# Head norms raised to a power on GpSimd, and later places for three returned inverses, in a hybrid decoder layer

## The chip, the cores and the metric

The kernel runs on one core of one Trainium2 chip. The time is device microseconds of one execution. The kernel before was timed in three runs: 1850.33, 1848.37 and 1849.48 us, median 1849.48.

## The reference

One layer of a decoder, for a prompt of 256 tokens and 8 single sampled tokens (264 columns in all), width 2048: a SwiGLU feed-forward net, a mixing layer, a second feed-forward net, and a final norm. The mixing layer projects to 38 blocks of 128 columns; half of its heads do sliding-window attention, the other half RWKV-7 time mixing: per head a state matrix that is carried from token to token.

```
    S, y = wkv_scan(wkv0, r, logw, k, v, kk, a)
    mean = jnp.mean(y, axis=-1, keepdims=True)
    var = jnp.mean((y - mean) ** 2, axis=-1, keepdims=True)
    yn = ((y - mean) * lax.rsqrt(var + GN_EPS)).reshape(B, T, RWKV_WIDTH) * ln_w + ln_b
    ...
    out = (yn + bonus.reshape(B, T, RWKV_WIDTH)) * g
```

The change concerns `rsqrt(var + GN_EPS)` of these 16 heads, which the kernel handles as 8 pairs of heads, each a tile of 128 partitions by 264 columns.

## The kernel before

Every large product (both feed-forward nets, the projections `win`, the output `wout`) goes through `gemm` (L154). It takes the weights in chunks of up to four 128x128 blocks. A chunk (L136) is loaded by SP into `raw`, rounded by ACT into `hi`, and the rest is taken by VectorE (DVE) into `lo`; TensorE (PE) then does three matmuls of 264 columns for each block, into a bank called `acc`. There are seven buffers each of `raw`, `hi` and `lo`, so that ACT and DVE can be at most seven chunks ahead of PE. The chunks run 1 to 1312 over the program: 544 in the first net, 152 for the 38 blocks of `win`, 16, 32 and 32 in the three passes of `wout`, 536 in the second net.

All else in the mixing layer is written as generator tasks. After each chunk of `win` and `wout` a `tick` (L96) advances every living task by one `yield`, so that their small instructions are spread between the chunks:

- `prep` (L450): one pair of heads, from the projections to the 64x64 blocks `gm`.
- `chain` (L577): one batch of two pairs, four batches in all (0 to 3). It inverts triangular 32x32 matrices by 30 steps on DVE (tiles `X`, `Xt`, `st`), sends the result through memory (`sb`) into the tile `TT`, waits `RWAIT` ticks (L616), transposes `TT` on DVE into `TN` (L620), builds the 64x64 inverses, walks the four chunks of time (tiles `N`, `Z`, `S`), and ends with the norms.
- `gnorm` (L744): the norm of a pair: on PE the centred `y`, ACT squares it, PE sums the squares, ACT takes the square root (L752), DVE the reciprocal (L753), and DVE multiplies (L754). Two more DVE operations with weight, bias, bonus and gate follow (L739, L740).
- `attend` (L790) and `dec_attend`: the attention heads, with softmax over DVE (maximum, reciprocal), ACT (exponential) and GpSimd (POOL; a product at L787).

DVE's instructions in a tick keep the order in which the program writes them (L57 to L62): a DVE instruction of one task that waits holds up those of all tasks behind it. The instructions of `chunk` are exempt when they are written with high priority (L138); Tile's scheduler decides where they and all other instructions stand on each engine's queue, by its own reckoning of when operands are ready. After that each engine works its queue strictly in order.

Before a pass of `wout` (L958) the heads that it needs have to be done: pass 0 takes batches 0 and 1, pass 1 four attention heads' tiles and batch 2, pass 2 batch 3 and the other four. The matmuls of a pass need the `hi` and `lo` of these (`split`, L947: `s<-y` and `s<-o`).

Of the kernel before, what the change touches and what calls it, by code (L numbers as in the profile page):

```python
# [9 lines left out]
AF = mybir.ActivationFunctionType  # L10
ALU = mybir.AluOpType
AX = mybir.AxisListType

P = 128
NP = 256
NB = 8
T = NP + NB
# [13 lines left out]
NWARM = 7  # L31
NGM, NKR, NUV, NTT, NBT = 10, 5, 3, 2, 5
NSTEP = 2
DWAIT, RWAIT = (10, 9, 8, 8), (12, 11, 9, 10)
PW = (2, 1, 3, 2, 2)
ALPHA = math.exp(-0.5)
LKV = 26
# [10 lines left out]
def body(tc, I, O):  # L48
    nc = tc.nc
    A, G, TE, SP = nc.scalar, nc.gpsimd, nc.tensor, nc.sync  # L50
# [13 lines left out]
    V, inside = Ordered(), [False]  # L64

    def tt(e, out, a, b, op):
        return e.tensor_tensor(out=out, in0=a, in1=b, op=op)  # L67
# [4 lines left out]
    def ts(e, out, a, s1, op0, s2=None, op1=None):  # L72
        k = {} if op1 is None else dict(op1=op1)
        e.tensor_scalar(out=out, in0=a, scalar1=s1, scalar2=s2, op0=op0, **k)

    def act(out, in_, f, **k):
        return A.activation(out=out, in_=in_, func=f, **k)  # L77

    def bc(ap, shape):
        return ap.broadcast_to(list(shape))  # L80

    def mm(out, lhsT, rhs, start=True, stop=True, **k):
        TE.matmul(out, lhsT, rhs, start=start, stop=stop, **k)  # L83
# [27 lines left out]
    def pause(n):  # L111
        for _ in range(n):
            yield

    with ExitStack() as ctx:
# [10 lines left out]
        def tmp(shape=(P, T), dt=F32):  # L126
            pool, n = cur[0]
            return pool.tile(list(shape), dt, tag="t", bufs=n, name=uid("t"))
# [4 lines left out]
        def mp():  # L133
            return pp.tile([P, 512], F32, tag="m", bufs=NM, name=uid("m"))
# [38 lines left out]
        eps = cp.tile([P, 2], F32, name="eps")  # L173
# [209 lines left out]
        def mixing(n2, n3, XD):  # L383
            with tc.tile_pool(name="mx", bufs=1) as mx:
                cur[0] = (mx, NT)
                return mixing_body(mx, n2, n3, XD)

        def mixing_body(mx, n2, n3, XD):
            def fix(shape, name):
                return mx.tile(list(shape), F32, name=name)  # L390
# [18 lines left out]
                G.memset(pj[:, 0:1], 0.0)  # L409
            nmu = fix((P, NSH), "nmu")  # L410
            mu = vec[:, VMU:VMU + NSH]
            nka = fix((P, NPAIR), "nka")
            ts(G, nka, vec[:, VKA:VKA + NPAIR], -1.0, ALU.mult)
            ts(V, nmu, mu, -1.0, ALU.mult, 1.0, ALU.add)
# [162 lines left out]
            def chain(bt):  # L577
# [10 lines left out]
                for g in range(ng):  # L588
                    r = slice(g * nr, (g + 1) * nr)
# [81 lines left out]
                for k in range(n):  # L671
                    for c in range(1, 4):
                        x = (k * 3 + c - 1) * 64
                        for h in range(2):
                            r = HALF[h]
                            mm(pP[HALF[1 - h], x:x + 64], W[r, k, c - 1, :], bt.BT[k][r, c, r])
                        for h in range(2):
                            r = HALF[h]
# [7 lines left out]
                for k in range(n):  # L686
                    for c in range(4):
                        x = (k * 4 + c) * 64
                        for h in range(2):
                            r = HALF[h]  # L690
                            mm(pN[r, x:x + 64], bt.BT[k][:, c, r], uv[:, c, k, r])
                for k in range(n):
                    for c in range(4):
                        x = (k * 4 + c) * 64
                        for h in range(2):
                            r = HALF[h]
# [7 lines left out]
                for c in range(1, 4):  # L704
                    ps = mp()
                    for k in reversed(range(n)):
                        for h in range(2):
                            r = HALF[h]
                            mm(ps[r, k * 64:k * 64 + 64], PT[r, k, c - 1, :], S[r, k])
                        for h in range(2):  # L710
                            r = HALF[h]
# [16 lines left out]
                g2s = [load(I["g2"][bt.p0 + k], (P, P)) for k in range(n)]  # L728
                gps = []
                gs = [gnorm(Ys[k]) for k in range(n)]  # L730
                for _ in range(PW[3] + 1):
                    for g in gs:
                        next(g)
                    yield
# [9 lines left out]
            def gnorm(y):  # L744
                yp = mp()
                mm(yp[:, :T], cm, y)
                r = tmp()
                act(r, yp[:, :T], AF.Square)
                yield from pause(PW[3])
                vp = mp()  # L750
                mm(vp[:, :T], bo, r)
                act(r, vp[:, :T], AF.Sqrt, scale=1.0 / 64, bias=eps[:, 1:2])  # L752
                V.reciprocal(r, r)  # L753
                tt(V, y, yp[:, :T], r, ALU.mult)  # L754
                yield

# [150 lines left out]
            for kind, i in SEQ:  # L907
                if kind == "b":
                    bt = newbatch(i)
                    for k in range(BATCH[i]):  # L910
                        p = bt.p0 + k
                        x = [shifted(2 + 3 * p + j, tmp()) for j in range(3)]
                        spawn(prep(p, bt, k, *x))
                    bat.append(spawn(chain(bt)))
                    bts.append(bt)
                    if len(bat) == len(BATCH):
# [209 lines left out]
```

## Time and profile before

| | us |
|---|---|
| median of three runs | 1849.48 |
| the profiled execution, its own time | 1849.28 |
| its span in the profile | 1847.5 |
| PE busy | 1823.9 |
| DVE busy | 1317.1 |
| ACT busy | 1068.6 |
| POOL busy | 258.7 |

The profile is one execution; its time is 0.2 us from the median, and 1.8 us of it lie outside of the span. A group's row gives line, engine, operation, output and inputs by name, shapes, count, then busy time and mean ns of one, then the idle time of the engine just before them and what ended it. A row of windows gives for a stretch (from:to, us) its length, the busy time and number of instructions of PE, PEld (weight loads), DVE, ACT and POOL, the granted clock of PE (1.00 is full), the DMA share and GB/s. Line 60 is the helper through which all DVE operations go, line 77 that of ACT's functions, line 67 that of `tensor_tensor` on POOL, line 83 that of matmuls: groups are told apart by their tiles.

### The profile page before, as it was taken

Reading aid. Unit: us, or ns where it says so; the run is one execution under the profiler, and the core shown is the slowest. Engines: PE = TensorE matmul, PEld = TensorE weight load, DVE = VectorE, ACT = ScalarE, POOL = GpSimd, SP = SyncE. Lnnn points to the kernel's source line nnn. Section 1 sums busy time; section 2 is a strip of 40 time slices with the busy share of each in tenths; the row PEclk is TensorE's granted clock in tenths of the full one; section 3 lists DMA queues with packets and bytes.
Section 4 is the critical chain, followed back from the end, with each engine's and each line's share of the span. In section 5 each row is a group of like instructions: output and inputs, shape, how many; then the busy total and the mean of one; then the engine's idle time right before and its main releaser. Section 6 shows DMA issues by size and latency. Waiting matters only on the chain.

```text
span 1847.5 us, 46195 instructions
## 1 busy us (share of the span) xinstructions
PE 1823.9 (99%) x17212; PEld 1795.0 (97%) x17212; DVE 1317.1 (71%) x2613; ACT 1068.6 (58%) x2134; POOL 258.7 (14%) x389
## 2 busy tenths in 40 slices
PE   9999999999999999999998999999999999999998
PEld 9999999999999999999997899999999999999997
DVE  6966666666656677799887687876766676667765
ACT  6645555455554567877766676654545555454555
POOL 0401001010010122222221200220101001010012
PEclk9999999999999999999999899999999999999999
DMA  8666666666666677555566356666666666666664
GB/s 274 191 204 211 196 212 205 202 198 188 205 190 201 196 203 241 177 169 152 164 177 177 118 148 213 186 201 190 203 206 208 195 208 205 203 207 193 215 190 137
DMA packets 226466, 358.25 MB, mean 194 GB/s; under 512 B 38441, under 2 KB 82113, under 8 KB 226241
## 3 DMA queue, kind: packets, MB, share of 16 engines
q1 hardware_dynamic: 220352, 349.20, 62.7%
q10 hardware_dynamic: 5888, 6.11, 1.1%
q8 instruction: 135, 2.21, 0.5%
q14 instruction: 91, 0.74, 0.1%
HBM read 347.06 MB, written 10.22 MB: 193 GB/s over the span
## 4 chain that ended last, share of the span: by engine, by line
PE 93%; DVE 2%; DMA 2%; issue 1%; ACT 1%; SPq 0%; POOL 0%; POOLq 0%; ACTq 0%; DVEq 0%
PE acc L83 85%; PE m L83 7%; DVE lo L60 1%; DMA raw<-in_gu 0%; DMA raw<-in_wout 0%; DMA sb<-Xt 0%; ACT t L77 0%; DVE t L60 0%; DMA X<-sa 0%; DMA TT<-sb 0%; DVE st L60 0%; ACT hi L147 0%; DVE Xt L60 0%; PE m L551 0%; DMA raw<-in_win 0%
## 5 line engine op out<-in xcount | busy, mean ns | idle before, releaser
L60 DVE TENSOR_TENSOR lo<-raw,hi 128x512 fp32r<-128x512 f32 (+2 forms) x1312 | 884.5, 678 | 439.9 <-ACT hi L147 410.9
L147 ACT CAST hi<-raw 128x512 fp32r<-128x512 f32 (+2 forms) x1312 | 775.9, 596 | 665.8 <-PE acc L83 446.7
L83 PE MATMUL acc<-s,hi 128*128 128x264 f32 x5940 | 1034.1, 278 | 3.4 <-ACT s L950 2.2
L83 PEld LDWEIGHTS acc<-s,hi 128*128 128x128 f32 x5940 | 901.1, 189 | 9.5 <-ACT s L950 2.6
L83 PE MATMUL acc<-s,lo 128*128 128x264 f32 x2970 | 824.3, 278 | 0.2 <-DVE lo L60 0.2
L83 PEld LDWEIGHTS acc<-s,lo 128*128 128x128 f32 x2970 | 562.2, 189 | 2.3 <-DVE lo L60 0.4
L83 PE MATMUL acc<-t,hi 128*128 128x264 f32 x2752 | 465.0, 276 | 0.0
L83 PEld LDWEIGHTS acc<-t,hi 128*128 128x128 f32 x2752 | 414.9, 189 | 0.0
L83 PE MATMUL acc<-t,lo 128*128 128x264 f32 x1376 | 379.2, 276 | 0.0
L67 POOL TENSOR_TENSOR t<-t,t 128x264 f32<-128x264 f32 (+1 forms) x148 | 140.6, 950 | 1068.7 <-ACT hi L147 986.0
L83 PEld LDWEIGHTS acc<-t,lo 128*128 128x128 f32 x1376 | 260.1, 189 | 0.0
L83 PE MATMUL acc<-y,hi 128*128 128x264 f32 x648 | 113.8, 277 | 0.0
L83 PEld LDWEIGHTS acc<-y,hi 128*128 128x128 f32 x648 | 97.8, 189 | 0.2
L83 PE MATMUL acc<-y,lo 128*128 128x264 f32 x324 | 89.4, 276 | 0.0
L60 DVE TENSOR_TENSOR t<-acc,t 128x264 f32<-128x264 f32 x156 | 67.3, 431 | 20.4 <-PE acc L83 12.0
L67 POOL TENSOR_TENSOR o<-o,o 128x264 f32<-128x264 f32 x43 | 35.9, 835 | 198.7 <-ACT o L77 192.6
L83 PEld LDWEIGHTS acc<-y,lo 128*128 128x128 f32 x324 | 61.2, 189 | 0.0
L83 PE MATMUL acc<-o,hi 128*128 128x264 f32 x324 | 58.8, 276 | 0.0
L83 PEld LDWEIGHTS acc<-o,hi 128*128 128x128 f32 x324 | 48.8, 189 | 0.0
L60 DVE SCALAR_TENSOR_TENSOR s<-acc,s 128x264 f32<-128x264 f32 x96 | 40.9, 430 | 8.9 <-PE acc L83 6.3
L300 ACT CAST t<-t 128x264 fp32r<-128x264 f32 x86 | 38.5, 447 | 13.5 <-POOL t L67 8.1
L83 PE MATMUL m<-s,hi 128*128 128x264 f32 x260 | 44.9, 277 | 0.2
(243 smaller groups left out, 1276.3 us busy)
## 6 DMA issues: line engine op xcount, KB each, us to landing
raw<-in_gu SPq DMA_DIRECT2D x680, 256.0 KB, 3.4
raw<-in_dn SPq DMA_DIRECT2D x224, 256.0 KB, 3.0
raw<-in_win SPq DMA_DIRECT2D x152, 256.0 KB, 3.6
raw<-in_dn SPq DMA_DIRECT2D x160, 192.0 KB, 2.7
raw<-in_wout SPq DMA_DIRECT2D x48, 256.0 KB, 3.3
raw<-in_wout SPq DMA_DIRECT2D x32, 128.0 KB, 2.5
s<-xsp SPq DMA_DIRECT2D x16, 132.0 KB, 3.5
raw<-in_gu SPq DMA_DIRECT2D x16, 128.0 KB, 3.3
```

Of the source, the lines that this page charges most:

```text
L60: i = getattr(nc.vector, name)(*a, **k)
L67: return e.tensor_tensor(out=out, in0=a, in1=b, op=op)
L83: TE.matmul(out, lhsT, rhs, start=start, stop=stop, **k)
L147: A.copy(hi[:, :w], raw[:, :w])
L300: A.copy(halves(hi), pairs(u))
```

## The change

The norm's variance gets its epsilon by a plain ACT operation (Identity: scale and bias), and GpSimd raises it to the power of -0.5, with a constant tile `half` that is read with stride zero. The square root and the reciprocal are gone. Between the power and DVE's product stand three more ticks, and the loop that drives the norms is three ticks longer. `RWAIT`, the ticks between the return of the inverses' diagonal blocks and their transposition, grows by 1, 2 and 8 for batches 1, 2 and 3.

```diff
-DWAIT, RWAIT = (10, 9, 8, 8), (12, 11, 9, 10)
+DWAIT, RWAIT = (10, 9, 8, 8), (12, 12, 11, 18)
...
+            half = fix((P, 1), "half")
+            G.memset(half, -0.5)
...
-                for _ in range(PW[3] + 1):
+                for _ in range(PW[3] + 4):
                     for g in gs:
                         next(g)
                     yield
...
-                act(r, vp[:, :T], AF.Sqrt, scale=1.0 / 64, bias=eps[:, 1:2])
-                V.reciprocal(r, r)
+                act(r, vp[:, :T], AF.Identity, scale=1.0 / 64, bias=eps[:, 1:2])
+                tt(G, r, r, bc(half, (P, T)), ALU.pow)
+                yield from pause(3)
                 tt(V, y, yp[:, :T], r, ALU.mult)
```

Over the whole program the built kernel has 8 reciprocals fewer on DVE, 9 loads of a function table fewer on ACT, and on POOL 8 `TENSOR_TENSOR t<-t,half` more (and one memset); PE and SP have the same instructions. What moves is their order. Three places show it. Line numbers of the changed kernel are two to three higher behind the edits.

On DVE before, behind the sums of squares of batch 0 (the pairs 0 and 1 have the tiles `y_13237` and `y_13238`; their variances are `t_13619` and `t_13623`; `lo` is the rest of a weight chunk):

```order
L60 TENSOR_TENSOR lo_14043<-raw_14041,hi_14042 128x512
L60 RECIPROCAL t_13619<-t_13619 128x264
L60 TENSOR_TENSOR lo_14093<-raw_14091,hi_14092 128x512
L60 TENSOR_TENSOR y_13237<-m_13617,t_13619 128x264
L60 RECIPROCAL t_13623<-t_13623 128x264
L60 TENSOR_TENSOR lo_14127<-raw_14125,hi_14126 128x512
L60 SCALAR_TENSOR_TENSOR y_13237<-y_13237,vec,t_11146 128x264
L60 TENSOR_TENSOR st_13935<-X_13683,Xt_13684 128x30
L60 TENSOR_TENSOR y_13238<-m_13621,t_13623 128x264
```

On DVE in the changed kernel, the second of these two products (its pair's tile is now `y_13240`) and what stands around it:

```order
L60 TENSOR_TENSOR lo_16524<-raw_16522,hi_16523 128x512
L60 TENSOR_TENSOR lo_16550<-raw_16548,hi_16549 128x512
L60 SCALAR_TENSOR_TENSOR o_16327<-acc_16181,rs 128x264
L60 TENSOR_TENSOR lo_16581<-raw_16579,hi_16580 128x512
L60 TENSOR_TENSOR y_13240<-m_13623,t_13625 128x264
L60 SCALAR_TENSOR_TENSOR t_13748<-t_13748,t_13747 128x264
L60 SCALAR_TENSOR_TENSOR y_13240<-y_13240,vec,t_11516 128x264
L60 TENSOR_TENSOR t_13748<-t_13748,t_13744 128x264
L60 SCALAR_TENSOR_TENSOR y_13240<-y_13240,vec,m_13855 128x264
L60 TENSOR_TENSOR st_13937<-X_13685,Xt_13686 128x30
```

Before, the first product stands behind chunk 648 and the second behind chunk 649, and the tasks go on at once (`st`, the inversion of batch 2). Now the first stands behind chunk 677 and the second behind chunk 703, and with it everything that the tasks still have for DVE: the inversion `st_13937` of batch 2, which stood three rows behind the first product, comes only here. Behind chunk 703 there are 126 DVE instructions in a row with no `lo` between them, behind chunk 719 there are 130, behind chunk 751 there are 21.

On PE before, the end of the last block of `win` and the start of pass 0 (`s_16405` is a split head):

```order
L83 MATMUL acc_16188<-s_10600,hi_16333 128x264
L83 MATMUL acc_16188<-s_10601,hi_16333 128x264
L83 MATMUL acc_16188<-s_10600,lo_16334 128x264
L83 MATMUL m_15904<-t_15745,s_14845 64x256
L83 MATMUL m_15904<-t_15809,s_14845 64x256
L83 MATMUL m_15904<-t_15746,s_14845 64x128
L83 MATMUL m_15904<-t_15810,s_14845 64x128
L816 MATMUL m_15932<-C,t_15756 128x128
L817 MATMUL m_15932<-C,t_15755 128x128
L818 MATMUL m_15932<-C,t_15755 128x128
L83 MATMUL acc_16421<-s_16405,hi_16423 128x264
```

On PE in the changed kernel, the end of the same block, and then the end of what stands ahead of pass 0 (149 rows of this stretch are left out):

```order
L83 MATMUL acc_16181<-s_10600,lo_16311 128x264
L83 MATMUL m_13943<-t_13820,C 128x280
L83 MATMUL m_13946<-XD,ld_13872 64x2 x2
...
L83 MATMUL m_14768<-t_14678,C 128x264
L83 MATMUL m_14772<-t_14682,C 128x264
L767 MATMUL m_14833<-C,s_14793 8x128
...
L83 MATMUL m_15033<-s_14339,o_14978 128x256
L83 MATMUL m_15033<-s_14339,o_14978 128x128
L83 MATMUL acc_16377<-s_16361,hi_16379 128x264
L83 MATMUL acc_16407<-s_16361,hi_16409 128x264
```

Before, 7 small matmuls stand between the last block of `win` and pass 0; now there are 243, from the preparation of pair 6 to the norms of batch 1. Ahead of them the 48 chunks that end with this block stand on PE without a single small matmul between them, where before small ones stood between almost all of them.

On DVE, the transposition of batch 3's returned inverses before, and that of batch 2's in the changed kernel:

```order
L60 RECIPROCAL stb_15761<-stb_15761 128x2
L60 STREAM_TRANSPOSE TN_16235<-TT_14798 32x256
L60 TENSOR_TENSOR stb_15819<-stb_15819,stc_15820 128x2
L60 RECIPROCAL stb_15819<-stb_15819 128x2
L60 TENSOR_TENSOR stb_15873<-stb_15873,stc_15874 128x2
L60 STREAM_TRANSPOSE TN_16235<-TT_14798 32x256
```

```order
L60 TENSOR_TENSOR Xt_13686<-Xt_13686,st_14687 128x8
L60 TENSOR_TENSOR gm_14641<-m_14631,C 128x512
L60 TENSOR_TENSOR gm_14690<-m_14632,C 128x512
L60 STREAM_TRANSPOSE TN_15073<-TT_13695 32x256 x2
L60 TENSOR_TENSOR s_14887<-acc_14795,rs 128x264
L60 TENSOR_TENSOR s_16362<-y_13239,s_16361 128x264
L60 TENSOR_TENSOR s_16366<-y_13240,s_16365 128x264
L60 TENSOR_TENSOR y_14289<-m_14676,t_14678 128x264
```

In the first, the transposition stands among the attention's softmax (`stb`). In the second, it stands two instructions behind the last step of the inversion (`Xt_13686`) whose result it is to read after the trip through memory, and ahead of the products of batch 1 (`y_14289`) that pass 0 needs. In ticks, batch 3's transposition goes from tick 150 to 158 and the end of its norms from 163 to 174, where pass 2 begins with tick 200.

## Prediction

> **What bounds the kernel now.** The page comes first: the shares of the engines and the chain that ended last.
>
> ```profile
> PE 1823.9 (99%) x17212; PEld 1795.0 (97%) x17212; DVE 1317.1 (71%) x2613; ACT 1068.6 (58%) x2134; POOL 258.7 (14%) x389
> PE 93%; DVE 2%; DMA 2%; issue 1%; ACT 1%; SPq 0%; POOL 0%; POOLq 0%; ACTq 0%; DVEq 0%
> ```
>
> PE works all the time, so an operation that leaves DVE or ACT is worth nothing by itself; time can only come from PE's 23.6 us of idleness, its clock, or be lost by making PE idle. The windows over the mixing layer's second half show where it idles.
>
> ```profile
> 885.00:1007.50 122.50, 119.63 (x1524) 109.95 (x1522) 105.79 (x326) 85.99 (x213) 25.14 (x50) 1.00 0.61 173
> 1007.50:1017.50 10.00, 2.20 (x12) 1.19 (x11) 4.56 (x26) 6.47 (x21) 1.71 (x4) 0.72 0.70 202
> 1017.50:1104.00 86.50, 85.80 (x946) 77.23 (x947) 64.64 (x196) 58.69 (x163) 14.21 (x28) 0.95 0.43 128
> 885.00:1104.00 219.00, 207.63 (x2481) 188.38 (x2480) 174.99 (x546) 151.15 (x397) 41.06 (x80) 0.97 0.55 157
> 1020.00:1030.00 10.00, 10.00 (x71) 8.32 (x69) 6.13 (x25) 5.64 (x18) 2.44 (x7) 0.72 0.30 87
> ```
>
> One hole, ahead of pass 0, holds 7.8 us of the idleness, and the clock stays low behind it. The timeline names the waits.
>
> ```profile
> 1014.40 0.47 PE L816 MATMUL m<-C,t 128*128 128x128 f32 x1 [5.25 <-ACT t L788]
> 1016.00 0.43 DVE L60 STREAM_TRANSPOSE TN<-TT 32x256 f32<-32x256 f32 x1 [3.57 <-DMA TT<-sb]
> 1017.53 1.03 PE L83 MATMUL acc<-s,hi 128*128 128x264 f32 x3 [2.23 <-ACT s L950]
> 1018.21 0.44 DVE L60 STREAM_TRANSPOSE TN<-TT 32x256 f32<-32x256 f32 x1 [1.48 <-DMA TT<-sb]
> ```
>
> DVE stands at batch 3's transposition, whose data is still on its way; softmax and the splits for pass 0 queue behind it, and PE waits for these. The edit of `RWAIT` aims at this hole.
>
> **The change, part by part.** The rows of what goes, and of what is nearest to what comes:
>
> ```profile
> L60 DVE RECIPROCAL t<-t 128x264 f32<-128x264 f32 x8 | 14.4, 1800 | 5.4 <-ACT t L77 5.4
> L77 ACT ACT_TABLE_LOAD x27 | 34.6, 1283 | 2.4 <-PE m L83 1.9
> L77 ACT ACTIVATE t<-m,eps 128x264 f32<-128x264 f32 x8 | 3.6, 480 | 0.1
> L67 POOL TENSOR_TENSOR t<-t,t 128x264 f32<-128x264 f32 (+1 forms) x148 | 140.6, 950 | 1068.7 <-ACT hi L147 986.0
> L60 DVE TENSOR_TENSOR y<-m,t 128x264 f32<-128x264 f32 x8 | 3.4, 424 | 0.0
> ```
>
> *Removed:* 8 x 1.80 = 14.4 us of DVE and 9 x 1.28 = 11.5 us of ACT; the ACT function itself stays (0.48 us, taken as equal). Neither engine is the bound, so this counts only inside stretches where PE waits for them.
>
> *Added:* 8 powers on POOL. No row shows one. Below: POOL's product of the same size, 0.95 us. From the nearest kind: DVE's reciprocal takes 1.80/0.424 = 4.2 times its product, and a power is a logarithm, a product and an exponential; at 4.2 products for each of the two functions it is 2 x 4.2 x 0.95 + 0.95 = 9 us. No row bounds it above; 32 us is the point at which the first pair of powers would be late too (two of them in the 66 us of the first stage below), and serves as the upper end. I take 9 us and keep 1 and 32.
>
> The Trainium skill (GPSIMD Engine Reference, 3.1) gives about 2.6 cycles for each element of a two-input operation on GpSimd and calls VectorE the right engine for elementwise work; if a power ran at that rate it would be an estimated 264 x 2.6 / 1.2 GHz = 0.6 us, and the sum below would be that of the cheap power. The trace agrees on products (0.95 against 0.42 us) and says nothing on powers.
>
> *Moved:* this decides. The queues shown above with the change say that DVE's product of batch 0's second pair now stands behind chunk 703, seven chunks into pass 0. The seven buffers let DVE get there only when PE has done the last chunk of `win`, and pass 0 itself needs batch 1, which stands behind that product. So the small work that was spread over the chunks now stands in three heaps, ahead of the three passes, with no chunk to fill PE meanwhile: 126, 130 and 21 DVE instructions (ACT: 94, 81, 13 between two casts), with the DMAs on SP that go between. That holds whatever a power costs, as each engine's order is fixed.
>
> The sum goes by stages from 885 us, where batch 0's variances are ready, to 1104 us, where pass 2 starts. For the small instructions I take the stretch's mean without the chunks' own:
>
> ```profile
> 0.00:885.00 885.00, 444.12 (x647) 1.00 0.67 200
> 885.00:1104.00 219.00, 64.86 (x103) 0.97 0.55 157
> 885.00:1104.00 219.00, 58.32 (x104) 0.97 0.55 157
> ```
>
> These are the `lo` on DVE up to 885 us (647 chunks) and after, and the `hi` on ACT: DVE (174.99 - 64.86)/(546 - 103) = 0.249 us for each small instruction, ACT (151.15 - 58.32)/(397 - 104) = 0.317 us, a `lo` 0.63 us. PE's pace, its pace behind the hole, and the trip through memory are in the chain of waits:
>
> ```profile
> 1099.57 39.38 PE acc L83 x350
> 1023.75 2.05 PE acc L83 x10
> 1011.07 3.04 DMA sb<-Xt
> 1015.58 2.60 DMA TT<-sb
> ```
>
> A matmul takes 39.38/350 = 0.1125 us, and 0.205 behind the hole.
>
> 1. The 49 chunks left of `win`, nothing between: 49 x 12 x 0.1125 = 66 us.
> 2. First heap: DVE alone 126 x 0.249 = 31 us; if DVE and ACT (94 x 0.317 = 30) took turns, 61. In it batch 1 goes from PE to ACT to DVE a dozen times, while batch 2's inversion and two preparations fill in: midway, 46. Batch 2's transposition now waits for its whole trip, 3.04 + 2.60 us, ahead of batch 1's products: 52. Ends 31 and 67.
> 3. Pass 0: 192 matmuls are 22 us, but DVE has 92 x 0.249 + 16 x 0.63 = 33 us. Ends 33 and 38.
> 4. Second heap (batch 2 and most of the attention): 130 x 0.249 = 32 us; in turns with ACT's 26 us, 58. Midway 45.
> 5. Pass 1: 288 matmuls 32 us, and some small ones between: 38. Ends 32 and 42.
> 6. Third heap: 5 us; in turns, 9: 7.
>
> Together 66 + 52 + 33 + 45 + 38 + 7 = 241 us against 219 now: +22. The hole of now is in the 219, so its end is in this; the added ticks of `RWAIT` bring nothing more, for ticks are worth time only while chunks run between them, and batch 2's transposition stands two instructions behind the end of its inversion. Batch 3's is now off PE's way. The later ends (batch 1 at tick 121, 2 at 143, 3 at 174) lie ahead of the passes (152, 168, 200), and cost nothing by themselves.
>
> PE's clock: today's hole costs some 4 us behind it (2.8 us in 1020 to 1030 at 0.72, and about half of the 2.5 us ahead of that). Three holes instead of one: +8. The Trainium skill (TensorE: Matmul & The Clock Gate, Part 1) has the clock halve after an idle window of about 3.4 us and come back after a busy one; the hole shows it (5.25 us idle, then 0.72). By this rule of the Trainium skill alone, heaps that keep PE ticking over with small matmuls might keep the clock, and the sum would be 8 us less.
>
> The powers: in each heap two follow each other on POOL ahead of the product that the pass waits for, 2 x 9 = 18 us, of which the trip of batch 2's inverses covers 6 in the first, and DVE's other rows 2 each in the others: 54 - 10 = +44.
>
> Sum: 1849.3 + 22 + 8 + 44 = **1923 us** by the profiled execution (1849.28, the median being 1849.48); rounded to 1925. For the range: with a power of 1 us, all covered, 1879; of 32 us, 1849.3 + 30 + 192 - 10 = 2061; all lower ends (66 + 31 + 33 + 32 + 32 + 5 = 199) without clock or powers 1829; all upper ends (66 + 67 + 38 + 58 + 42 + 9 = 280), clock, cheap power 1918.
>
> **The rivals.**
>
> *A cheap power.* POOL is idle 86% of the span and its products take under a microsecond; nothing on ACT or DVE has to wait for it then. Only the heaps are paid: 1879 us. For it: the one POOL row of this shape. Against: that row is a product.
>
> *A dear power: POOL is the bound.* At 32 us or more each, six of the eight stand in PE's way, one after the other: 2061 us, and 6 to 8 us more for each further microsecond. For it: between the variances and their products the new order leaves 29 and 26 chunks, as if much time were needed there; that is no time, but it is odd for a cheap operation. It decides from about 20 us on (1989 us).
>
> *Faster: the heaps run dense.* DVE has 20% of this stretch idle today, and the reciprocals go from it. If in the heaps DVE hardly ever waited, these took 69 us, and the whole stretch 199 instead of 219: 1829 us. It decides where the three heaps need less than 219 - 66 - 33 - 38 = 82 us, that is, DVE busy over 69/82 = 84% in them, with a cheap power. It has 80% today, with chunks to fill in; in the heaps there is none, and the steps of a batch wait for each other over three engines and a DMA trip. I hold it unlikely.
>
> *The change does what it says but its places don't:* this is in the sum, since the order shows it.
>
> **How the numbers follow.** A power of 4 to 20 us: 0.40 (the forecast, 1893 to 1989). Cheap: 0.24 (1855 to 1893). Dear: 0.26. Dense: 0.10. The range reaches from the cheap case's lower edge, 1855, to a power of some 38 us, 2095; that leaves out the dense case and the dearest tenth. A time within 0.2% (3.7 us, about what a measurement of this kernel can tell from no change) needs a stretch of 215 to 223 us: 0.04, from the seam of dense and cheap. Faster 0.08, slower 0.88.
>
> **What would show it.** In the profile after: some 66 us of PE from about 885 us on with nothing but `acc`; then a hole ahead of each pass in which PE does only small matmuls, at a lower clock, the first 40 to 70 us long; in the rows, POOL `t<-t,half` with its mean, and DVE's `y<-m,t` waiting for POOL twice the power's length. Wrong if the holes are missing or under 82 us together, or if the order on the chip spreads the small work over the chunks as before; the size stands or falls with the mean of the power.

## The result, and the profile after

The changed kernel takes 2128.87 us (median of 4 runs, 2127.17 to 2131.41), the kernel before on the same chip 1849.74 us (4 runs, 1848.37 to 1850.33): 1.1512 times as long, 95% interval 1.1499 to 1.1526. The forecast was 1925, with a range up to 2095.

The page of the kernel after: span, engines, the bars of PE, POOL and PE's clock, and the chain that ended last.

```profile
span 2128.4 us, 46202 instructions
PE 1854.7 (87%) x17212; PEld 1815.8 (85%) x17212; DVE 1305.0 (61%) x2605; ACT 1061.8 (50%) x2125; POOL 593.6 (28%) x398
PE   9999999999999999996234183199999999999998
POOL 1201010101011222493976927802110110101012
PEclk9999999999999999996667587599999999999999
PE 80%; POOL 8%; issue 6%; DVE 3%; DMA 1%; ACT 1%; SPq 0%; POOLq 0%; ACTq 0%; DVEq 0%
```

The span grew by 280.9 us. PE has the same 17212 matmuls, and its busy time grew by only 31 us; so most of the loss is idleness of PE. The bars of PE and POOL are mirror images from slice 19 to slice 26, counted from 1 (a slice is 53 us): the fuller POOL is, the emptier is PE. POOL, which had 0% of the chain before, now has 8% of it, some 170 us.

The groups of instructions of the kernel after; L67 is POOL's power, L60 DVE's product with it, L953 the split for a pass, L83 the pass's matmuls:

```profile
L67 POOL TENSOR_TENSOR t<-t,half 128x264 f32<-128x264 f32 x8 | 339.9, 42498 | 39.8 <-ACT t L77 39.6
L60 DVE TENSOR_TENSOR y<-m,t 128x264 f32<-128x264 f32 x8 | 3.5, 431 | 238.6 <-POOL t L67 238.6
L953 ACT CAST s<-y 128x264 fp32r<-128x264 f32 x8 | 3.2, 430 | 110.4 <-DVE y L60 109.6
L83 PE MATMUL acc<-s,hi 128*128 128x264 f32 x5940 | 1032.9, 279 | 76.5 <-ACT s L953 75.9
```

One power takes 42.5 us, 8 of them 339.9. DVE's eight products took 0.43 us each and stood idle 238.6 us ahead of them, all of it for the power; before, the same row had no idle time. Behind three of the late products the split waits on ACT (109.6 us), and PE on the split (75.9 us); behind the others PE waits for DVE directly. That is the chain of the loss, link by link; the waits of its links overlap and are not added.

The timeline of the kernel after shows the powers on POOL (start, length; two rows in one are two powers back to back) ...

```profile
883.88 42.47 POOL L67 TENSOR_TENSOR t<-t,half 128x264 f32<-128x264 f32 x1 [2.02 <-ACT t L77]
927.22 42.78 POOL L67 TENSOR_TENSOR t<-t,half 128x264 f32<-128x264 f32 x1
1013.40 84.85 POOL L67 TENSOR_TENSOR t<-t,half 128x264 f32<-128x264 f32 x2 [6.43 <-ACT t L77]
1139.88 42.47 POOL L67 TENSOR_TENSOR t<-t,half 128x264 f32<-128x264 f32 x1
1183.23 42.46 POOL L67 TENSOR_TENSOR t<-t,half 128x264 f32<-128x264 f32 x1
1292.48 84.88 POOL L67 TENSOR_TENSOR t<-t,half 128x264 f32<-128x264 f32 x2 [31.18 <-ACT t L77]
```

... and the products on DVE that wait for them:

```profile
970.04 0.43 DVE L60 TENSOR_TENSOR y<-m,t 128x264 f32<-128x264 f32 x1 [7.23 <-POOL t L67]
1055.88 0.43 DVE L60 TENSOR_TENSOR y<-m,t 128x264 f32<-128x264 f32 x1 [37.47 <-POOL t L67]
1098.28 0.43 DVE L60 TENSOR_TENSOR y<-m,t 128x264 f32<-128x264 f32 x1 [39.93 <-POOL t L67]
1182.38 0.43 DVE L60 TENSOR_TENSOR y<-m,t 128x264 f32<-128x264 f32 x1 [38.94 <-POOL t L67]
1225.72 0.43 DVE L60 TENSOR_TENSOR y<-m,t 128x264 f32<-128x264 f32 x1 [37.97 <-POOL t L67]
1334.98 0.43 DVE L60 TENSOR_TENSOR y<-m,t 128x264 f32<-128x264 f32 x1 [37.09 <-POOL t L67]
1377.40 0.43 DVE L60 TENSOR_TENSOR y<-m,t 128x264 f32<-128x264 f32 x1 [40.00 <-POOL t L67]
```

Each of these products starts 0.03 to 0.04 us behind the end of its power. Only batch 0's first power (883.88) is hidden: PE still works off `win` then. PE itself stands still for more than 20 us at six places, each time at the end of one of the six later powers, 227.6 us together; the row ahead of them is a shorter stop, for a small POOL operation behind batch 0's second power:

```profile
974.48 1.29 PE L83 MATMUL m<-t,C 128*128 128x280 f32 x2 [12.94 <-POOL t L67]
1056.37 1.65 PE L83 MATMUL m<-s,o 64*128 64x256 f32 x4 [36.30 <-DVE y L60]
1100.42 1.25 PE L83 MATMUL acc<-s,hi 128*128 128x264 f32 x4 [32.99 <-ACT s L953]
1182.87 1.25 PE L83 MATMUL m<-sgl,ld 128*128 128x264 f32 x2 [40.52 <-DVE y L60]
1226.30 0.44 PE L819 MATMUL m<-C,t 128*128 128x128 f32 x1 [37.51 <-DVE y L60]
1336.98 1.25 PE L83 MATMUL acc<-s,hi 128*128 128x264 f32 x4 [41.52 <-ACT s L953]
1378.04 0.69 PE L885 MATMUL m<-C,bk 128*128 128x128 f32 x2 [38.71 <-POOL bk L74]
```

The last of them waits for a small operation of another task (`bk`) that stands behind the power on POOL itself. The windows of the kernel after (columns as in the section on before) show what PE has meanwhile:

```profile
885.00:950.00 65.00, 65.00 (x572) 64.74 (x571) 38.66 (x63) 34.34 (x60) 64.86 (x4) 1.00 0.67 203
950.00:1384.00 434.00, 172.18 (x1925) 142.96 (x1923) 131.56 (x474) 109.68 (x325) 304.87 (x85) 0.65 0.17 50
1080.00:1100.00 20.00, 0.00 (x0) 0.00 (x0) 1.48 (x3) 0.06 (x1) 19.83 (x5) 0.50 0.00 0
1340.00:1360.00 20.00, 0.00 (x0) 0.00 (x0) 0.00 (x0) 0.00 (x0) 20.00 (x1) 0.50 0.00 0
```

In the last one POOL works alone in the whole core; in the one above it DVE and ACT have four instructions beside POOL. In both there is no DMA and no matmul, and PE's clock stands at 0.50. The Trainium skill (TensorE: Matmul & The Clock Gate, Part 1) has the clock halve in an idle stretch; these rows agree.

### The profile page after: what moved, and what is told of

Read it like the earlier page. It is cut to its first block, busy times and chain, and to the rows that moved or that the text cites. A ratio compares the mean times of both kernels' runs of the same rounds, so it can differ in the third digit from the quotient of the medians.

```text
span 2128.4 us, 46202 instructions
## 1 busy us (share of the span) xinstructions
PE 1854.7 (87%) x17212; PEld 1815.8 (85%) x17212; DVE 1305.0 (61%) x2605; ACT 1061.8 (50%) x2125; POOL 593.6 (28%) x398
## 4 chain that ended last, share of the span: by engine, by line
PE 80%; POOL 8%; issue 6%; DVE 3%; DMA 1%; ACT 1%; SPq 0%; POOLq 0%; ACTq 0%; DVEq 0%
PE acc L83 74%; POOL t L67 8%; PE m L83 6%; DMA raw<-in_gu 1%; DVE t L60 0%; DVE st L60 0%; DVE Xt L60 0%; ACT t L77 0%; DVE lo L60 0%; ACT hi L147 0%; DVE s L60 0%; DVE y L60 0%; PE m L553 0%; DMA raw<-in_win 0%; DVE bk L60 0%
## 5 line engine op out<-in xcount | busy, mean ns | idle before, releaser
L60 DVE TENSOR_TENSOR lo<-raw,hi 128x512 fp32r<-128x512 f32 (+2 forms) x1312 | 875.8, 672 | 476.6 <-ACT hi L147 446.3
L83 PE MATMUL acc<-s,hi 128*128 128x264 f32 x5940 | 1032.9, 279 | 76.5 <-ACT s L953 75.9
L83 PEld LDWEIGHTS acc<-s,hi 128*128 128x128 f32 x5940 | 904.0, 190 | 82.1 <-ACT s L953 76.8
L83 PE MATMUL acc<-s,lo 128*128 128x264 f32 x2970 | 824.9, 278 | 0.0
L83 PEld LDWEIGHTS acc<-s,lo 128*128 128x128 f32 x2970 | 564.6, 190 | 2.0 <-issue 1.1
L83 PE MATMUL acc<-t,hi 128*128 128x264 f32 x2752 | 465.0, 276 | 0.0
L67 POOL TENSOR_TENSOR t<-t,t 128x264 f32<-128x264 f32 (+1 forms) x148 | 146.3, 989 | 1062.6 <-ACT hi L147 996.0
L83 PEld LDWEIGHTS acc<-t,hi 128*128 128x128 f32 x2752 | 414.9, 189 | 0.0
L83 PE MATMUL acc<-t,lo 128*128 128x264 f32 x1376 | 379.2, 276 | 0.0
L67 POOL TENSOR_TENSOR t<-t,half 128x264 f32<-128x264 f32 x8 | 339.9, 42498 | 39.8 <-ACT t L77 39.6
L83 PEld LDWEIGHTS acc<-t,lo 128*128 128x128 f32 x1376 | 260.1, 189 | 0.0
L60 DVE TENSOR_TENSOR y<-m,t 128x264 f32<-128x264 f32 x8 | 3.5, 431 | 238.6 <-POOL t L67 238.6
L83 PE MATMUL acc<-y,hi 128*128 128x264 f32 x648 | 113.8, 277 | 0.0
L83 PEld LDWEIGHTS acc<-y,hi 128*128 128x128 f32 x648 | 97.8, 189 | 0.2
L67 POOL TENSOR_TENSOR o<-o,o 128x264 f32<-128x264 f32 x43 | 35.7, 830 | 196.5 <-ACT o L77 189.7
L83 PE MATMUL acc<-y,lo 128*128 128x264 f32 x324 | 89.4, 276 | 0.0
L60 DVE TENSOR_TENSOR t<-acc,t 128x264 f32<-128x264 f32 x156 | 67.2, 431 | 20.7 <-PE acc L83 12.4
L83 PEld LDWEIGHTS acc<-y,lo 128*128 128x128 f32 x324 | 61.2, 189 | 0.0
L83 PE MATMUL acc<-o,hi 128*128 128x264 f32 x324 | 58.8, 276 | 0.0
L953 ACT CAST s<-y 128x264 fp32r<-128x264 f32 x8 | 3.2, 430 | 110.4 <-DVE y L60 109.6
L83 PEld LDWEIGHTS acc<-o,hi 128*128 128x128 f32 x324 | 48.8, 189 | 0.0
```

The source lines that it names most:

```text
L60: i = getattr(nc.vector, name)(*a, **k)
L953: A.copy(halves(hi), m)
```

## The experiments

The theory (A) behind all of them: the power itself takes 42.5 us on POOL, DVE's in-order queue waits for it, and six to seven of the eight stand in PE's way. The rivals: the cost is in what surrounds it (the values, the constant that is read with stride zero, the hop over POOL), in the changed order with its heaps, or in the places of `RWAIT`. Where one time alone is given, it is that of one execution and has no interval; the kernel before took 1849.15 to 1849.97 us (medians) beside them.

**Values.** The exponent is 0 in place of -0.5, so the norm's division is left out.

```diff
-            G.memset(half, -0.5)
+            G.memset(half, 0.0)
```

> The changed kernel with the exponent 0 instead of -0.5, so that the norm is left out (the variance becomes 1); the order of all instructions is that of the changed kernel. Theory A (a power on GpSimd costs 42.5 us by its columns, whatever the values; six of the eight stand in PE's way): 2129 us, the power's mean 42.5 us. Rival B (its time depends on the values, the exponent 0 being an easy one): a shorter mean, and with a power near 1 us the heaps of small work alone remain, 1880 to 1895 us.

Measured: 2126.84 us. Its group row:

```profile
L67 POOL TENSOR_TENSOR t<-t,half 128x264 f32<-128x264 f32 x8 | 339.9, 42497 | 39.6 <-ACT t L77 39.4
```

With the exponent 0, where every result is 1, a power takes as long as before, and so does the kernel. Theory A's 2129 us holds, and the rival's short power does not come.

**Half of the columns.** The power is taken on 132 of 264 columns; the rest keep the plain variance.

```diff
-                tt(G, r, r, bc(half, (P, T)), ALU.pow)
+                tt(G, r[:, :T // 2], r[:, :T // 2], bc(half, (P, T // 2)), ALU.pow)
```

> The power on the first 132 of 264 columns alone; the others keep the plain variance, so half of the norm is left out. Theory A: the mean of the power falls to 21.3 us; by the prediction's sum with that power (1879 - 10 + 6 x 21.3) 1997 us, somewhat less because the order now has one heap instead of two long ones (DVE: 128 instructions behind chunk 719, none behind 703): 1960 to 2000. Rival C (a fixed cost of each power, such as loading its code): mean near 42.5 us and 2100 us or more.

Measured: 1969.22 us, span 1967.4. Group row, and DVE's line in the table of waits (us in total, times, longest):

```profile
L67 POOL TENSOR_TENSOR t<-t,half 128x132 f32<-128x132 f32 x8 | 171.3, 21421 | 39.9 <-ACT t L77 39.7
```
```profile
DVE y L60 <- POOL t L67: 101.8, 6, 19.2
```

From 21.42 and 42.50 us: 0.16 us for each column and 0.34 us beside them, so the rival's fixed cost is not there. The kernel's time follows, inside Theory A's range: (2128.87 - 1969.22)/(42.50 - 21.42) = 7.6 us for each microsecond of a power. Not all of this is waiting for powers, since the order changed too (behind chunk 703 there are 17 DVE instructions in a row, not 126; behind chunk 719 still 128). The waits account for (238.6 - 101.8)/21.08 = 6.5 us of the 7.6.

**A product in place of the power.** Same operands, same engine, same stride-zero read, all places kept; the norm gets the variance times -0.5 in place of its root's inverse.

```diff
-                tt(G, r, r, bc(half, (P, T)), ALU.pow)
+                tt(G, r, r, bc(half, (P, T)), ALU.mult)
```

> A product on GpSimd with the same tile in place of the power (the norm's scale is wrong by that; all else as in the changed kernel). Theory A: the product takes 0.9 to 1 us, the order has no heaps, DVE loses 14.4 us and ACT 11.5 us, and batch 3's transposition does not stop DVE ahead of pass 0 any more: 1836 to 1848 us. Rival D (the hop over GpSimd and the added ticks themselves cost, not the power's length): above 1860 us.

Measured: 1845.31 us (10 runs, 1844.53 to 1847.46), inside Theory A's range; ratio to before 0.9980, interval 0.9970 to 0.9989. Its group row, and the window in which the hole of before lies:

```profile
L67 POOL TENSOR_TENSOR t<-t,half 128x264 f32<-128x264 f32 x8 | 5.0, 623 | 31.0 <-ACT t L77 30.9
```
```profile
1000.00:1020.00 20.00, 20.00 (x188) 16.70 (x188) 13.20 (x51) 14.04 (x46) 6.42 (x6) 1.00 0.70 209
```

The product takes 0.62 us, the power 68 times that. Operand, hop and ticks cost nothing that can be seen; with an operation as cheap as this product the change would gain 0.2%, and PE has no hole ahead of pass 0. One thing here goes beyond the price: the built order of this kernel has no heaps, though its text differs in one word. In its trace at most 23 DVE instructions stand between two `lo` (before 30, after 130). So the heaps, too, come with the power. Their length changes with the power's columns (126 and 130 for all of them, 17 and 128 for a half, 33 and 74 for a quarter). It looks as if the scheduler reckons with a long operation and lays the order around it; its own reckoning is not on record.

**The places alone.** Root and reciprocal are put back as before; the new `RWAIT` and the added ticks stay.

```diff
-                act(r, vp[:, :T], AF.Identity, scale=1.0 / 64, bias=eps[:, 1:2])
-                tt(G, r, r, bc(half, (P, T)), ALU.pow)
+                act(r, vp[:, :T], AF.Sqrt, scale=1.0 / 64, bias=eps[:, 1:2])
+                V.reciprocal(r, r)
                 yield from pause(3)
```

> Root and reciprocal back, with all added ticks kept (RWAIT 12, 12, 11, 18, three more ticks in the norm). Theory A (places): the hole of 7.8 us ahead of pass 0 closes partly or wholly, 1838 to 1850 us. Rival E (the later end of the batches, with 37 DVE instructions in a row behind chunk 703 instead of 30, stops pass 0 for longer): 1850 to 1862 us.

Measured: 1853.57 us (9 runs, 1851.46 to 1856.0), ratio 1.0022, interval 1.0012 to 1.0032. The window of the old hole:

```profile
1020.00:1040.00 20.00, 16.69 (x154) 13.24 (x153) 13.66 (x57) 13.37 (x47) 7.01 (x14) 0.91 0.77 235
```

The old place of the hole (1000 to 1020 us) is full now, a smaller hole stands here, and the kernel is slightly slower than before: in Rival E's range, outside Theory A's. In the profiles PE's idleness is 0.8 us less than before, and its busy time for the same matmuls 6.2 us more (1830.1 against 1823.9); why is open.

**One partition.** The power on 1 of 128 partitions, meant to leave the order and take the price away (the other 127 keep the plain variance).

```diff
-                tt(G, r, r, bc(half, (P, T)), ALU.pow)
+                tt(G, r[0:1], r[0:1], bc(half[0:1], (1, T)), ALU.pow)
```

> The power on one of the 128 partitions alone (the rest of the tile keeps the plain variance, so the norm is left out for it). Every engine's order is word for word that of the changed kernel. If a power costs by its columns whatever the partitions: 42.5 us and 2127 us again. If it costs by partitions as well: a short power in the same order, and the time shows the heaps of small work alone; the changed kernel's profile puts them at 2128.4 - 238.6 (the waits for powers) - 1847.5 = 42 us, so 1885 to 1895; the prediction's sum had 30 us (1879), and the rival of dense heaps 1829 to 1849.

Measured: 2128.13 us.

```profile
L67 POOL TENSOR_TENSOR t<-t,half 1x264 f32<-1x264 f32 x8 | 339.8, 42486 | 39.7 <-ACT t L77 39.6
```

At 264 columns, 1 partition costs as much as 128: the price goes by columns. So this kernel could not do what it was for: after's order with a cheap power was not had, and the heaps' own cost is not measured apart.

**The power with the old places.**

```diff
-DWAIT, RWAIT = (10, 9, 8, 8), (12, 12, 11, 18)
+DWAIT, RWAIT = (10, 9, 8, 8), (12, 11, 9, 10)
```

> The power and its ticks kept, RWAIT back to 12, 11, 9, 10. Theory A (the added places bring nothing where ticks run without chunks): 2120 to 2135 us. Rival (the places shorten the waits for the returned inverses in the heaps): 2140 us or more.

Measured: 2113.54 us, span 2111.7, 6 us under the range of Theory A and further from the rival's. The table of waits and POOL's last rows in the timeline:

```profile
DVE y L60 <- POOL t L67: 203.5, 7, 40.9
```
```profile
1010.51 84.85 POOL L67 TENSOR_TENSOR t<-t,half 128x264 f32<-128x264 f32 x2 [3.78 <-ACT t L77]
1134.36 84.87 POOL L67 TENSOR_TENSOR t<-t,half 128x264 f32<-128x264 f32 x2
1275.68 85.00 POOL L67 TENSOR_TENSOR t<-t,half 128x264 f32<-128x264 f32 x2 [10.44 <-ACT t L77]
```

Against after, the pairs of powers start 2.9, 5.5 and 16.8 us earlier (1013.40, 1139.88, 1292.48 there), and the spans differ by 16.7. So the new places did not help against the powers: they cost 15 to 17 us, of which the last pair (batch 3, moved by 8 ticks) has 11. The waits for powers fell by 35 us here, twice as much as the span, so these waits are no price that can simply be subtracted.

**A longer pause.** 26 ticks between power and product in place of 3, with the old `RWAIT`: can the distance hide the power?

```diff
-                for _ in range(PW[3] + 4):
+                for _ in range(PW[3] + 27):
...
-                yield from pause(3)
+                yield from pause(26)
```

> 26 ticks instead of 3 between the power and its product, RWAIT as before the change. Theory A (POOL works in order: the copies of the preparations and the softmax products stand behind 85 us of powers, so ticks cannot hide them): the waits move from DVE's product to others, the order has 266 DVE instructions in a row behind chunk 703, and the time stays above 2000 us. Rival (more places hide the powers): under 1950 us.

Measured: 2138.55 us, as Theory A has it. From the table of waits:

```profile
PEld m L885 <- POOL bk L74: 83.2, 1, 83.2
PE m L820 <- POOL t L74: 80.9, 2, 40.7
DVE y L60 <- POOL t L67: 65.8, 3, 41.4
```

DVE's wait for the powers fell from 203.5 to 65.8 us, and the loss stayed: a matmul's weights now wait 83.2 us for `bk`, a 0.6 us operation of another task that stands behind a pair of powers on POOL (two powers are 85 us), and two matmuls of the attention wait 80.9 us for its products there (`t`, L74). POOL works in order here, as DVE does. Ticks move the wait from one queue to the other.

**Another form of the same norm.** Before's places; the logarithm and `exp(-0.5 ln)` on ACT take the place of root and reciprocal, so DVE loses the reciprocals and POOL gets nothing.

```diff
-                act(r, vp[:, :T], AF.Sqrt, scale=1.0 / 64, bias=eps[:, 1:2])
-                V.reciprocal(r, r)
+                act(r, vp[:, :T], AF.Ln, scale=1.0 / 64, bias=eps[:, 1:2])
+                act(r, r, AF.Exp, scale=-0.5)
```

> The kernel before with logarithm and exponential on ACT (exp(-0.5 ln)) in place of root and reciprocal, nothing else moved. It takes 14.4 us from DVE, adds 8 x 0.45 us to ACT and, by its order, 7 table loads of 1.28 us (40 instead of 33). If DVE's reciprocals are what delays pass 0: 1840 to 1847 us. If the table loads on ACT weigh as much: 1848 to 1855 us.

Measured: 1849.3 us (10 runs, 1847.98 to 1849.76), ratio 0.9996, interval 0.9986 to 1.0006. The loads of function tables in the kernel before, and in this one (the prediction's row with 27 of them covers a part of the program):

```profile
L77 ACT ACT_TABLE_LOAD x33 | 42.3, 1283 | 3.2 <-PE m L83 1.9 <-PEq L1118 0.7
L77 ACT ACT_TABLE_LOAD x40 | 51.3, 1283 | 3.2 <-PE m L83 1.9 <-PEq L1118 0.7
```

7 more table loads on ACT and 14.4 us less on DVE make no difference. The old place of the hole is nearly full here, first the kernel before, then this one:

```profile
1000.00:1020.00 20.00, 11.50 (x99) 9.32 (x98) 13.02 (x52) 10.49 (x32) 3.99 (x7) 0.80 0.70 205
1000.00:1020.00 20.00, 19.84 (x175) 17.44 (x174) 14.85 (x58) 11.98 (x38) 3.59 (x6) 0.84 0.62 178
```

Still PE's idleness over the whole span is 22.3 us and was 23.6: it lies at other places. A hole that closes is not yet time gained.

**The places, one by one.** In the kernel before, `RWAIT` alone: batch 3's place (first), batches 1 and 2 (second), and all places with `exp(-0.5 ln)` (third).

```diff
-DWAIT, RWAIT = (10, 9, 8, 8), (12, 11, 9, 10)
+DWAIT, RWAIT = (10, 9, 8, 8), (12, 11, 9, 18)
```

> The kernel before with one place moved: batch 3's returned inverses wait 18 ticks in front of their transposition and not 10. Theory A (the places of themselves bring nothing or cost a little, as all of them together did with the root and the reciprocal: ratio 1.002): 1848 to 1854 us. Rival (one of the places is worth something and another costs it): below 1846 us.

Measured: 1859.13 us (4 runs, 1857.87 to 1861.22), ratio 1.0054, interval 1.0040 to 1.0068.

```diff
-DWAIT, RWAIT = (10, 9, 8, 8), (12, 11, 9, 10)
+DWAIT, RWAIT = (10, 9, 8, 8), (12, 12, 11, 10)
```

> The kernel before with the other two places alone: batches 1 and 2 wait 12 and 11 ticks (before 11 and 9), batch 3 ten as before. Since batch 3's place alone costs 10 us and all three with the three ticks cost 4, Theory A (these two places give back some 4 to 6 us): 1843 to 1847 us, a version faster than both kernels. Rival (they bring nothing, and the three ticks or the joint order made the difference): 1848 to 1854 us.

Measured: 1853.34 us (11 runs, 1848.64 to 1855.34), ratio 1.0016, interval 1.0007 to 1.0025.

```diff
-DWAIT, RWAIT = (10, 9, 8, 8), (12, 11, 9, 10)
+DWAIT, RWAIT = (10, 9, 8, 8), (12, 12, 11, 18)
...
-                act(r, vp[:, :T], AF.Sqrt, scale=1.0 / 64, bias=eps[:, 1:2])
-                V.reciprocal(r, r)
+                act(r, vp[:, :T], AF.Ln, scale=1.0 / 64, bias=eps[:, 1:2])
+                act(r, r, AF.Exp, scale=-0.5)
```

> The kernel before with the root as exp of -0.5 times the logarithm on ACT, no reciprocal on DVE, and the new places (12, 12, 11, 18). Theory A (without a slow power, and with 8 reciprocals fewer on DVE, the places can be used, as with the product on GpSimd, ratio 0.998): 1844 to 1848 us. Rival (what the product's kernel gained hung on the three ticks or on its own order): 1849 to 1854 us, as with the root and the new places.

Measured: 1853.29 us (11 runs, 1852.72 to 1854.27), ratio 1.0021, interval 1.0012 to 1.0030. The first lies above Theory A's range and far from the rival's, so both were wrong there; in the other two the rival's range held. Neither batch 3's place nor the other two gain by themselves, and they do not add up (batch 3's place alone costs 10 us, with the other places and other norms 4). In the kernel with batch 3's place the old hole ahead of pass 0 stays (3.29 us of PE in 10, before 2.20) and a second one comes. First the kernel before, then that kernel:

```profile
1085.00:1120.00 35.00, 35.00 (x323) 34.68 (x322) 29.95 (x74) 23.71 (x54) 1.78 (x5) 1.00 0.62 194
```
```profile
1007.50:1017.50 10.00, 3.29 (x41) 2.16 (x33) 5.32 (x28) 5.75 (x19) 1.24 (x4) 0.80 0.74 216
1085.00:1120.00 35.00, 31.52 (x285) 29.15 (x284) 24.43 (x59) 21.26 (x51) 1.19 (x5) 0.95 0.43 127
```

Only the kernel with the product gained; whether that hangs on its three ticks, on POOL's part in it or on the order that came of both stays open. No kernel here that computes the reference beats the kernel before.

**A quarter of the columns.** The power on 66 columns, 198 keep the plain variance: its price is near the forecast's 9 us, so this tries the rest of the sum.

```diff
-                tt(G, r, r, bc(half, (P, T)), ALU.pow)
+                tt(G, r[:, :T // 4], r[:, :T // 4], bc(half, (P, T // 4)), ALU.pow)
```

> The changed kernel with the power on 66 of the 264 columns, so that 198 columns keep the plain variance. By the two sizes measured the power takes 10.9 us, near the 9 us of the prediction. Theory A (the rest of the prediction's sum holds, only the price was wrong): 1849.3 + 22 + 8 + 6 x 10.9 - 10 = 1935 us, 1920 to 1950. Rival (a wait of this size is mostly hidden by the seven chunks that stand ready and by an order with fewer heaps): 1855 to 1905 us; a straight line through the whole and the half gives 1890.

Measured: 1887.95 us, span 1886.2. Group row, table of waits, and the window of the deepest hole:

```profile
L67 POOL TENSOR_TENSOR t<-t,half 128x66 f32<-128x66 f32 x8 | 87.8, 10977 | 39.3 <-ACT t L77 39.1
```
```profile
DVE y L60 <- POOL t L67: 22.1, 4, 8.5
```
```profile
1040.00:1060.00 20.00, 8.11 (x77) 4.87 (x77) 8.67 (x41) 7.51 (x29) 12.50 (x6) 0.66 0.18 49
```

The rival was right: 47 us under the sum. Of eight powers of 11 us only four, those of batches 2 and 3, are waited for, 22.1 us in all, where the sum has 6 x 10.9 - 10 = 55; and heaps and clock took 1886.2 - 1847.5 - 22.1 = 17 us, where it has 30. Its order is another, too: DVE's heaps behind chunks 703 and 719 have 33 and 74 instructions, after's 126 and 130.

## Why the prediction was wrong, point by point

**The step that failed is the price of the power**: "I take 9 us and keep 1 and 32." A power takes 42.5 us. DVE's ratio of a reciprocal to a product said nothing of POOL: its power is 45 times the 0.95 us product of the row that was used, and 68 times the product with the same operands. The upper end, 32 us, was no bound of the price but a point where the mechanism turns, and the prediction said that no row bounds it above; the range yet left out "the dearest tenth" from 38 us on. The 0.6 us estimated from the Trainium skill (GPSIMD Engine Reference, 3.1) agree with the product as measured in the same place (0.62 us), are about half of a product of two full tiles (1.12 us), and are far from the power.

**With the measured price its own sum comes near, in part by luck.** 1849.3 + 22 + 8 + 6 x 42.5 - 10 = 2124 us; batch 0's second power, late from 32 us on as the dear rival has it, adds its 7.23: 2131.5 against 2128.9. The closeness comes from errors that cancel (the next paragraphs have them), and at 11 us the same sum was 47 us too high. The rival "a dear power: POOL is the bound" is what happened, by its mechanism and its place, and it had been given 0.26. Its slope, "6 to 8 us more for each further microsecond", is 7.6 between the half and the whole.

**The stages.** `win` ends on PE at 961.5 us (the stop of 12.94 us up to 974.48 begins there). The other stages end where PE goes on in full with a pass: pass 0 has its first matmuls, on batch 0's heads, from 1017.65 us on, but stops for batch 1 until 1100.42; pass 1 starts at 1245; pass 2 starts at 1336.98 and goes on in full at 1384. PE's matmuls into `acc` from 885 us to the end of `win`, busy time and number:

```profile
885.00:962.00 77.00, 74.96 (x653) 1.00 0.66 202
```

| stage | us after | waits for powers in it | left | forecast |
|---|---|---|---|---|
| `win`, 885 to 961.5 | 76.5 | 0 | 76.5 | 66 |
| first heap, to 1100.4 | 138.9 | 84.6 | 54.3 | 52 |
| pass 0 and second heap, to 1245 | 144.6 | 76.9 | 67.7 | 78 |
| pass 1 and third heap, to 1384 | 139 | 77.1 | 61.9 | 45 |
| together | 499 | 238.6 | 260.4 | 241 |

The third column adds DVE's waits from the timeline above; the forecast's stages leave out its 8 us for the clock. The first stage is 10 us too short in the forecast: it counts 49 chunks from DVE's 647 `lo`, but at 885 us PE has 653 matmuls left, which are 54 chunks at 12 each. By DVE's waits, heaps and clock together took 2128.4 - 1847.5 - 238.6 = 42 us, not 30, and the powers 238.6 us, where six of 42.5 less 10, and the 7.23, are 252. This split is an account and not a measurement: in the kernel with the power and the old places the same subtraction leaves 61 us (2111.7 - 1847.5 - 203.5).

PE's own account points at the clock as a further term that was mis-sized. PE is 250.1 us more idle than before, 227.6 of them in its six long waits; the other 22.5 are near the forecast's 22 for the heaps, but the stop of 12.94 us behind batch 0's second power is among them. PE's busy time for the same 17212 matmuls grew by 30.8 us, at a clock of 0.65 over the 434 us. If all of that growth is the clock's, it cost some 31 us, an estimate from these numbers, where the sum has 8.

**"That holds whatever a power costs"** was right of the order that was built, and wrong as a thought about causes: with a product the heaps are not there, and with 66 columns they are small. The 29 and 26 chunks between variance and product, "odd for a cheap operation", fit a scheduler that holds the power for long. The prediction had this clue, put it down as "no time", and gave it too little weight.

**"The added ticks of `RWAIT` bring nothing more"** was right in sign of no gain and too mild: 15 us lost beside the powers (2128.87 against 2113.54), and 0.2% with root and reciprocal, interval 0.1 to 0.3%. Why batch 3's place costs time stays open.

**Dense heaps** and **a cheap power** did not happen; the product's kernel shows what lay behind them: 1845.31 us, where the cheap rival had 1879, since the heaps that it paid for are not there.

## What to carry to other kernels

Before moving an operation to another engine, look for a row of that very function there, or measure it by itself: a product's row says nothing of a power's price. Read the built order as evidence too: where it leaves tens of microseconds of other work between a new instruction and its reader, as it did here, the scheduler may hold that instruction to be as long. And an operation of 42 us on an engine that is idle 86% of the time is no free work when both that queue and its reader's run in order: here, distance between the two only moved the wait to whatever else stood behind it.

## What was unexpected in the hardware

- POOL's power costs by its columns: 10.98, 21.42 and 42.50 us for 66, 132 and 264 columns of 128 partitions, and 42.49 us for 264 columns of one.
- It takes the same time with exponent 0 as with -0.5 (42.50 us each).
- POOL's product with the stride-zero operand was quicker than the one of two full tiles with the same output. The kernel with the product, its groups with shapes apart:

```profile
L67 POOL TENSOR_TENSOR t<-t,t 128x264 f32<-128x264 f32 x74 | 83.0, 1122 | 1016.8 <-ACT hi L147 986.0 <-DVE t L60 18.0 <-PE acc L83 10.3
```

With the stride-zero operand it took 0.62 us there, with two full tiles 1.12; no run here shows why.
